# An ifftshift of 8192 x 8192 floats by DMA alone: part of the copies moved to the other queue and cut into 8 KB packets

## The chip, the cores and the metric

The kernel runs on one core of a Trainium2 chip. Its time is the device time in microseconds (us) of one execution, given as the median of several runs. The core has compute engines (none of which this kernel uses for the result), and sixteen DMA engines that move data. Two of the core's instruction streams issue the DMAs here: SyncE (SP in the profile) and ScalarE (ACT). A DMA is split over the sixteen DMA engines; each moves its share in packets, one packet for one contiguous run of bytes. The profile calls the sync engine's queue q1 and the scalar engine's queue q10.

## The reference

```python
def setup_inputs():
    return {"x": np.random.randn(8192, 8192).astype(np.float32)}

def reference(x):
    return np.fft.ifftshift(x)
```

For even sizes this swaps the quadrants: output row r, column c is input row (r + 4096) mod 8192, column (c + 4096) mod 8192. No arithmetic is done. The matrix has 268.44 MB, so the kernel reads and writes 268.44 MB each. A row is 32 KB, half a row 16 KB, and every half row of the output is a contiguous half row of the input.

## The kernel before, in words

The kernel copies from HBM to HBM with DMAs only; `copy` (line 26) works out the source of an output region and issues one DMA for it (line 29) on the queue that it is given. `hr` and `hc` are half the rows and half the columns, `ENGINES` is 16 and `per` is 16, so a block is `rows` = 256 rows and the output has 32 blocks. Of each block the left half (columns 0 to 4095) and the right half are two copies of 4 MB each.

The pattern `back` (line 45) describes a half block as 16 x 16 half rows of 16 KB. Its outer dimension, one step of one row, is what is split over the sixteen DMA engines; its inner dimension goes backward by 16 rows. So engine e copies row e of every group of sixteen rows: at any time the sixteen engines work on about sixteen neighbouring rows, from the block's last group to its first.

The loops (lines 47 to 54) go through the blocks from the last to the first in groups of four. The left halves all go to the sync queue in falling order (line 49). The right halves all go to the scalar queue, with the order in each group of four turned by two (line 50). So each queue carries half of the bytes, in 16 KB packets.

One group of sixteen rows of one right half (`start`, line 36) is copied ahead of the loop, in column strips of 4 KB (lines 38 to 42). The strips are cut at 14, 9 and 4 rows into two DMAs each, so that the sixteen engines get different numbers of 4 KB packets, from one to seven. The scalar queue has seven such small DMAs ahead of its 32 large ones, of which one is a group shorter (`rest`, lines 46 and 52).

The order in which the DMAs are recorded is not yet the order in which they depend on each other. The framework (the tile context) puts the DMAs of both queues into one order of its own, hands eight completion semaphores out in turn along it, and lets each DMA wait, on the engine that issues it, until the DMA eight places earlier in that order has landed. Each engine issues its own DMAs strictly in that order. In the kernel before, the order is the first strip, the first sync DMA, the six other strips, and from there one scalar and one sync DMA in turn, so that after the start each queue has four DMAs outstanding and waits only for its own.

Of the kernel before, what the change touches and what calls it, by code (L numbers as in the profile page):

```python
# [1 line left out]

# [4 lines left out]


ENGINES = 16


@with_exitstack
def kernel(
    ctx: ExitStack,
    tc: tile.TileContext,
    x: bass.AP,
    out: bass.AP,
):
    nc = tc.nc
    R, C = x.shape  # L20
    hr = R // 2
    hc = C // 2
    per = 16
    rows = ENGINES * per

    def copy(queue, row, col, dims):

        src = (row + hr) % R * C + (col + hc) % C
        queue.dma_start(
            out=bass.AP(out.tensor, out.offset + row * C + col, dims),  # L30
            in_=bass.AP(x.tensor, x.offset + src, dims),
        )

    start = R - 3 * rows
    strip = hc // 4
    for n, k in enumerate((14, 9, 4)):
        col = hc + n * strip
        copy(nc.scalar, start + rows - ENGINES, col, [[C, k], [1, strip]])  # L40
        copy(nc.scalar, start + rows - ENGINES + k, col, [[C, ENGINES - k], [1, strip]])
    copy(nc.scalar, start + rows - ENGINES, hc + 3 * strip, [[C, ENGINES], [1, strip]])


    back = [[C, ENGINES], [-ENGINES * C, per], [1, hc]]
    rest = [[C, ENGINES], [-ENGINES * C, per - 1], [1, hc]]
    for first in range(R - 4 * rows, -1, -4 * rows):
        for n in (3, 2, 1, 0):
            copy(nc.sync, first + n * rows + rows - ENGINES, 0, back)
            right = first + (n + 2) % 4 * rows  # L50
            if right == start:
                copy(nc.scalar, right + rows - 2 * ENGINES, hc, rest)
            else:
                copy(nc.scalar, right + rows - ENGINES, hc, back)


# [1 line left out]
_INS = ['x']  # L58
_OUTS = [((8192, 8192), 'float32')]


# [23 lines left out]
```

## Time and profile before

| what | value |
|---|---|
| timed runs | 821.81, 822.63, 822.93 us; median 822.63 |
| the profiled execution: span from the first to the last instruction | 810.9 us |
| what lies around the span, by the median | 11.7 us |
| busy time of compute engines | POOL 0.2 us, four constants that the framework sets |
| DMA issues | sync 32 of 4,096 KB; scalar 31 of 4,096 KB, one of 3,840 KB and seven strips |
| first issue, on both queues | 0.73 us from the span's start |
| one issue instruction | median 571 ns on SP, 578 ns on ACT |
| from issue to landing on the sync queue | median 100.9 us |

The profile is that of one execution; of it the span is known, and the 11.7 us are the difference to the median of the timed runs. The page gives, for forty slices of the span, the mean busy share of the DMA engines (9 is 90% or more) and the GB/s that they copied, and for each queue its packets, its MB and the time of its packets as a share of sixteen engines' span. The view of stretches gives for any window of time its length, the busy time of POOL, the TensorE clock, the DMA share and, in the last column, the GB/s; it counts a packet in the window in which it starts, so that the share can stand a little over 1 in a short window. The records of single packets give the queue, start, duration and size of each, without the engine's number.

### The profile page before, as it was taken

What the parts mean: (1) busy time and instruction counts of PE and PEld (TensorE: products, weight loads), DVE (VectorE), ACT (ScalarE), POOL (GpSimd) and SP (SyncE); (2) the same over time, 40 slices, a digit from 0 to 9 for tenths busy, and PEclk for the clock granted to TensorE, in tenths of its full rate; (3) what the DMA queues carried; (4) which work ended last, traced back from release to release, by engine and by line L of the source; (5) the groups of instructions that cost most, each with busy time, mean ns of one, the idle gap of its engine ahead of it and who ended that gap; (6) DMA issues with size and microseconds to landing.
All of it is one profiled execution on the core that took longest, in us unless ns stands there. A gap on an engine that the chain in (4) does not pass through costs nothing. (4 is left out here: it accounts for less than half of the span.)

```text
span 810.9 us, 116 instructions
## 1 busy us (share of the span) xinstructions
POOL 0.2 (0%) x4
## 2 busy tenths in 40 slices
POOL 0000000000000000000000000000000000000000
DMA  9999999999999999999999999999999999999998
GB/s 302 328 335 329 334 333 331 331 335 330 326 331 329 331 335 330 332 332 337 335 336 333 333 337 330 334 335 331 336 331 333 335 334 335 333 330 336 333 338 296
DMA packets 17520, 268.44 MB, mean 331 GB/s; under 512 B 1088, under 2 KB 1088, under 8 KB 1152
## 3 DMA queue, kind: packets, MB, share of 16 engines
q1 hardware_dynamic: 8704, 134.22, 49.7%
q10 hardware_dynamic: 8816, 134.22, 49.6%
HBM read 268.44 MB, written 268.44 MB: 662 GB/s over the span
## 5 line engine op out<-in xcount | busy, mean ns | idle before, releaser
L69 POOL MEMSET const-bfloat16-1.0<- 128x1 bf16 x1 | 0.1, 102 | 0.0
L69 POOL MEMSET const-uint8-127<- 128x1 uint8 x1 | 0.1, 102 | 0.0
L69 POOL MEMSET const-float32-0.0<- 128x1 f32 x1 | 0.1, 99 | 0.2 <-issue 0.2
L69 POOL MEMSET const-float32-1.0<- 128x1 f32 x1 | 0.1, 99 | 0.0
## 6 DMA issues: line engine op xcount, KB each, us to landing
out_dram<-in_x_dram SPq DMA_DIRECT2D x32, 4096.0 KB, 100.9
out_dram<-in_x_dram ACTq DMA_DIRECT2D x31, 4096.0 KB
out_dram<-in_x_dram ACTq DMA_DIRECT2D x1, 3840.0 KB
out_dram<-in_x_dram ACTq DMA_DIRECT2D x1, 64.0 KB, 10.8
out_dram<-in_x_dram ACTq DMA_DIRECT2D x1, 56.0 KB
out_dram<-in_x_dram ACTq DMA_DIRECT2D x1, 48.0 KB
out_dram<-in_x_dram ACTq DMA_DIRECT2D x1, 36.0 KB
out_dram<-in_x_dram ACTq DMA_DIRECT2D x1, 28.0 KB
```

Source lines behind the costliest of these rows:

```text
L69: nc = _bacc.Bacc("TRN2", target_bir_lowering=False, num_devices=1)
```

## The change

The strips, the groups of four and the pattern `rest` go. The loop now runs over all 32 blocks from the last to the first. The left half of block n is copied as before, by `whole`, on the sync queue. The right half that goes with it is that of the block sixteen further on. When n leaves a remainder of 1 by 3 (11 of the 32 blocks) it is copied by `whole` as well, also on the sync queue. Otherwise (21 blocks) it is copied by `pieces` on the scalar queue: 256 rows in rising order, with the bytes of one packet limited to `piece * 4` = 8 KB, so that each half row is two packets. In the built program such a DMA has the dimensions 256 x 2 x 2048, in which the outermost is split over the engines: engine e gets sixteen rows in a row, e * 16 and on.

```diff
     per = 16
     rows = ENGINES * per
+    blocks = R // rows
+    piece = hc // 2
 
-    def copy(queue, row, col, dims):
-
+    def copy(queue, row, col, dims, **how):
         src = (row + hr) % R * C + (col + hc) % C
         queue.dma_start(
             out=bass.AP(out.tensor, out.offset + row * C + col, dims),
             in_=bass.AP(x.tensor, x.offset + src, dims),
+            **how,
         )
 
+    def whole(block, col):
+        dims = [[C, ENGINES], [-ENGINES * C, per], [1, hc]]
+        copy(nc.sync, block * rows + rows - ENGINES, col, dims)
 
+    def pieces(block):
+        copy(nc.scalar, block * rows, hc, [[C, rows], [1, hc]], max_dma_last_dim=piece * 4)
 
-    start = R - 3 * rows
-    strip = hc // 4
-    for n, k in enumerate((14, 9, 4)):
-        col = hc + n * strip
-        copy(nc.scalar, start + rows - ENGINES, col, [[C, k], [1, strip]])
-        copy(nc.scalar, start + rows - ENGINES + k, col, [[C, ENGINES - k], [1, strip]])
-    copy(nc.scalar, start + rows - ENGINES, hc + 3 * strip, [[C, ENGINES], [1, strip]])
-
-
-    back = [[C, ENGINES], [-ENGINES * C, per], [1, hc]]
-    rest = [[C, ENGINES], [-ENGINES * C, per - 1], [1, hc]]
-    for first in range(R - 4 * rows, -1, -4 * rows):
-        for n in (3, 2, 1, 0):
-            copy(nc.sync, first + n * rows + rows - ENGINES, 0, back)
-            right = first + (n + 2) % 4 * rows
-            if right == start:
-                copy(nc.scalar, right + rows - 2 * ENGINES, hc, rest)
-            else:
-                copy(nc.scalar, right + rows - ENGINES, hc, back)
+    for n in reversed(range(blocks)):
+        right = (n + blocks // 2) % blocks
+        whole(n, 0)
+        if n % 3 == 1:
+            whole(right, hc)
+        else:
+            pieces(right)
```

## The prediction

> **What bounds the kernel now.** I read three views, the page first. Its slices show the sixteen DMA engines busy from end to end and the bytes moving at an almost constant pace:
>
> ```profile
> DMA  9999999999999999999999999999999999999998
> DMA packets 17520, 268.44 MB, mean 331 GB/s; under 512 B 1088, under 2 KB 1088, under 8 KB 1152
> q1 hardware_dynamic: 8704, 134.22, 49.7%
> q10 hardware_dynamic: 8816, 134.22, 49.6%
> HBM read 268.44 MB, written 268.44 MB: 662 GB/s over the span
> ```
>
> No compute engine does anything. The two queues' shares add to 99.3% of sixteen engines, so an engine always has a packet in hand, and one at a time. The second view is the waits of the issuing engine:
>
> ```profile
> SPq L29 <- DMA out_dram<-in_x_dram: 686.8, 28, 28.4
> ```
>
> SP spends the span waiting for its own earlier DMAs. That is back-pressure, not starvation: four 4 MB DMAs per queue are outstanding, and an issue lands a median 100.9 us later while the queue finishes one about every 25 us. So an issue comes some 75 us before its bytes can move, and neither issue time nor the wait is on the path. The third view is the stretches of time:
>
> ```profile
> 3.00:5.00 2.00, 0.00 (x0) 1.00 0.96 393
> 5.00:14.00 9.00, 0.00 (x0) 1.00 1.03 338
> 14.00:23.00 9.00, 0.00 (x0) 1.00 1.02 327
> 30.00:780.00 750.00, 0.00 (x0) 1.00 1.00 333
> 805.50:808.50 3.00, 0.00 (x0) 1.00 0.94 311
> ```
>
> The last column is GB/s copied. In the trace's packet records a 16 KB packet takes 608 to 2346 ns, mean 786; a third of them take the smallest usual time, 611 ns, which on sixteen engines would be 429 GB/s. The steady 333 is therefore set by what the packets meet in memory, not by the engines. What they meet depends on which rows are in hand together: I spread each packet's bytes evenly over its duration and averaged the rate over all 25 us cycles between two completions on the sync queue. It runs from 304 to 362 GB/s with the place in the cycle, with a standard error of about 5 at each place. These two ends are my bounds for any arrangement that this trace does not show.
>
> **What the change really does: the order.** I followed the built order of the changed program, because eight completion semaphores are handed out in that order, and each DMA waits for the one eight places before it. Write A0 to A20 for the scalar DMAs and S0 to S42 for the sync DMAs. The order is A0, S0, A1 to A15, S1, A16 to A20, S2, S3, and so on to S42. So S1 waits for A8, S2 for A14, S3 for A15, S5 to S9 for A16 to A20, and SP issues strictly in order. The two queues are **not** interleaved 2:1 all through. The scalar queue runs first, almost by itself, and then the sync queue runs by itself.
>
> How many bytes move in which company follows from one 16 KB packet going beside one 8 KB packet (the records of before show the queues taking turns packet by packet, with chains of start and end on one engine). A sync DMA is then covered by half a scalar one. S0 and S1 each take half of an A; S2 takes half of A15; S3 and S4 fill A16; S5 to S8 each take half of one of A17 to A20. That makes 9 S and 4.5 A mixed (56.6 MB), 16.5 A alone (69.2 MB), and 34 S alone (142.6 MB). 79% of the bytes move with one queue alone, a state that before is in only at its two ends.
>
> **The terms**, against the profiled span of 810.9 us; the median of the timed runs, 822.63, lies 11.7 us above it, and I add the same 11.7 at the end.
>
> 1. Sync alone, 142.6 MB. The nearest row is 5 to 14 us, where the sync queue moves 16 KB packets beside a few 4 KB ones: 338 by the row, 332 when packets are cut at the window's edges. Bounds 304 and 362, that is +41 and -34 us against 428.2 us at 333. I take 332: **+1.3 us**.
>
> 2. Scalar alone, 69.2 MB. The nearest rows are 14 to 23 us, where the first sync DMA has ended and the second has no packet out yet (327; 322 cut at the edges from 16.5 to 22.3), and the last microseconds, scalar alone (311; 325 cut at the edges). I take 323: 214.2 instead of 207.8 us, **+6.4 us**. At 304 it is +20, at 362 it is -17. The engines' shares of a DMA also lie differently: before, sixteen engines work on sixteen neighbouring rows, 32 KB apart; now each has a block of sixteen rows, so neighbours are 512 KB apart. No row shows that spacing, so it gets the same two ends.
>
> The Trainium skill ("DMA: Bandwidth & Descriptors", section "Latency and other measured facts") states that copies within HBM lose rate with a row pitch at a large power of two: 207 instead of 214 GB/s per direction at 512 KiB, and far more from 2 MiB. Taken over to the spacing of the engines it would be an estimate of 3.4% on the scalar queue's 88.1 MB, +8.9 us in the place of +6.4, and 837 us in all. This trace has no such stretch.
>
> 3. 5,376 half rows become two packets each. From the records, 4 KB takes 159 ns uncontended and 16 KB 611, so a packet has (4 x 159 - 611) / 3 = 8.3 ns that does not grow with its bytes. 5,376 x 8.3 / 16 engines = 2.8 us if all of it shows, nothing if the memory hides it as it hides most of the difference between 611 and 786. I take the middle, **+1.4 us**.
>
> 4. The handover. S8 needs only half of A20's length, so when A20 ends the sync queue is empty, and S9 waits for A20. All engines stand still from their own last byte until A20's slowest has landed (a DMA's sixteen landings at the end of before are spread over 1.5 us, so about 0.8 in the mean), and then for the time from an issue to the first packet (issue at 0.73, first packet at 2.18 us: 1.45), and about 0.1 for the semaphore: **+2.4 us**. Bounds 0, if the packets' turns leave some of S8 over, and 4.
>
> 5. Nothing, with its cover: the seven strips go (0.6 to 1.4 us of issue each on ACT, while the sync queue was feeding all engines). The first packet still comes from an issue at the start. The instructions that issue (0.57 us each, 64 instead of 71) lie beside 12 us and more of data each; without that cover 64 of them on two queues would be under 25 us. The uneven strips gave engines 1 to 7 extra packets of 4 KB; the last landings were spread over 1.5 us, so at most that much comes back at the end, and I count none. ACT now issues eight DMAs ahead instead of four; if its ring cannot take them, only ACT's own issues are delayed, 50 us before they are needed. Each end of a DMA costs the queue one turn, which the other queue fills today; alone, the queue's own next packet should follow its 9 ns semaphore write.
>
> Sum: 810.9 + 1.3 + 6.4 + 1.4 + 2.4 = 822.4, and with 11.7 around it **834 us**, 1.4% slower than before.
>
> **Rivals.**
>
> *The rows collide* (chance 0.24). The 512 KB spacing, or one stream reading one half of each row and writing the other, meets memory as in the bad part of the cycle. For: around the end of a sync DMA the engines hold about thirteen scalar packets to three, and the rate falls to 304 to 318. Against: the 327 of 14 to 23 us. Scalar alone at 304 gives 834 + 13 = 847; both alone at 304 give 834 + 13 + 40 = 887.
>
> *One stream is better than two* (0.25; this one is faster than before). If packets of two unrelated row groups hinder one another, the lone sync queue runs freer: after the handover all engines restart together on sixteen neighbouring rows, as at launch. For: 393 from 3 to 5 us, and about 365 around the end of a scalar DMA, where thirteen packets of sixteen are the sync queue's. Against: the rate falls to 338 and below as soon as the launch is over, with the sync queue still nearly alone. At 362 the 142.6 MB take 394 instead of 429.5 us: 798 us; with the scalar part at 362 too, 775. It wins as soon as the lone sync queue holds more than 341 GB/s, which repays the 10.2 us of the other terms.
>
> *Company does not matter* (0.09). All bytes go at 333 in whatever queue, and only terms 3 and 4 are left: 826; if these too are hidden, 823, no change. The flat slices speak for it, the 304 to 362 within a cycle against it. The Trainium skill (same page, section "Issuing engines are not separate DMA queues") says the same as a rule: DMAs from different engines end on the same sixteen DMA engines and interleave, and a second issuing engine saves only issue time. The launch row of 338 agrees with it, the cycle does not.
>
> That the diff fails to bring the interleaving it describes is no rival here but part of the forecast. Were the queues after all to run 2:1, it would be term 3 alone, about 824.
>
> **How the numbers follow.** Forecast 0.42 (826 to 845), collision 0.24, one stream 0.25, no matter 0.09. A measurement of this kernel can tell about 0.2% from no change, 1.6 us. Faster: 0.25. Same: 0.06, the hidden part of the last rival. Slower: 0.42 + 0.24 + 0.03 = 0.69. The range of 792 to 874 leaves out the better half of the one-stream case below its 798, and the collision of both queues toward 887; the forecast's own range is 826 to 845.
>
> **What would show it.** Right order: q1 holds about 180 MB and q10 88 MB, with 10,752 packets of 8 KB on q10; ACT's issues all come in the first half, and SP's second one only after some 100 us; SP waits for DMAs for most of the first half. Handover: one dent in the DMA slices near the middle. Terms 1 and 2: GB/s of the slices at about 332 in the second half and 323 in the first. The forecast is wrong if the lone sync half stands above 341 or below 320, or if the queues share the whole span.

## The result and the profile after

The changed kernel takes 832.81 us (median of 4 runs, 828.19 to 834.8), the kernel before 822.78 beside it. The ratio is 1.0117, 95% interval 1.008 to 1.0153: slower by about 10 us. In a later set (experiment e7 below) it was 829.67 beside 821.42, ratio 1.0101 (1.0071 to 1.0131).

The page of the profile after, span 829.4 us:

```profile
DMA  8999999999999999998999999999999999999998
GB/s 297 320 328 325 332 325 327 330 317 333 330 328 331 327 323 331 324 326 290 318 320 314 329 319 330 322 327 331 329 325 327 326 327 327 323 332 329 327 328 292
DMA packets 22784, 268.44 MB, mean 324 GB/s; under 512 B 1024, under 2 KB 1024, under 8 KB 1024
...
q1 hardware_dynamic: 11696, 180.36, 65.7%
q10 hardware_dynamic: 11088, 88.08, 33.0%
HBM read 268.44 MB, written 268.44 MB: 647 GB/s over the span
```

The engines still have a packet in hand nearly all the time, so the loss is one of pace and of one hole. Of the bytes, two thirds are on q1 and one third on q10, as the diff says. The nineteenth slice (373 to 394 us) has the hole: 8 instead of 9, and 290 GB/s; the slices behind it stay at 314 to 330 for a while. The waits of the sync engine show the order (us in total, times, longest):

```profile
SPq L33 <- DMA out_dram<-in_x_dram: 382.1, 8, 131.1
```

and so do the issues in the view of line 33 (shortest, median and longest issue in ns, first and last start in us):

```profile
L33 SPq DMA_DIRECT2D out_dram<-in_x_dram x43: 571/11591/29097, 0.7 to 750.6; - x43
L33 ACTq DMA_DIRECT2D out_dram<-in_x_dram x21: 662/12602/37307, 0.7 to 269.4; - x21
```

SP waits in eight places only, once for 131 us: it holds one DMA and then stands until the scalar queue's A8 has landed. All scalar issues start in the first 270 us. In the packet records the scalar queue is alone for about 211 us and moves 68.6 MB in that time, both move for about 172, and the sync queue is alone from 389 us to the end.

One number of the prediction's base has to be read anew. Every timed run of the changed kernel stands 1.8 us above its own span, and so does the kernel before when it is profiled again (e0: 824.29 beside 822.5). With the same 1.8 us, the 810.9 us of the profile before belong to an execution of about 812.7 us (worked out, not measured), faster than any of its timed runs; not 11.7 us but 1.8 lie around a span. The sum was made of differences and then set upon the median, so it is not shifted by this. But 333 GB/s is the pace of that one execution; e0 has 327 to 329.

### The profile page after: what moved, and what is told of

It reads as the page before. It is cut to its first block, busy times and chain, and to the rows that moved or that the text cites. A ratio compares the mean times of both kernels' runs of the same rounds, so it can differ in the third digit from the quotient of the medians.

```text
span 829.4 us, 109 instructions
## 1 busy us (share of the span) xinstructions
POOL 0.2 (0%) x4
## 3 DMA queue, kind: packets, MB, share of 16 engines
q1 hardware_dynamic: 11696, 180.36, 65.7%
q10 hardware_dynamic: 11088, 88.08, 33.0%
```

## The experiments

All ratios are to the kernel before, run on the same chip in the same set, with their 95% interval. There are three sets, each on a chip of its own: e0 to e3, e4 to e7, e8 to e11. Each stretch that is shown is from one profiled execution of its version. The experiments that keep or change the order do it with edges between the DMAs that order them in the program and add no wait:

```diff
+        if issued:
+            tc.add_manual_dep(
+                dma.ins, issued[-1].name,
+                mybir.DependencyInfo(mybir.DependencyClass.NoSync, mybir.DependencyReason.DATA),
+                reason="order",
+            )
+        issued.append(dma.ins)
```

### e0: the kernel before against itself

No edit.

> The kernel before, unchanged, against itself. The profile that the prediction worked from had a span of 810.9 us, while the timed runs of the changed kernel stand only 1.8 us above their spans, so the 810.9 belongs to an execution of about 812.7 us, some 10 us under the median of 822.8. Theory: executions of this kernel scatter by about 1%, and a new profile will show a span of 815 to 825 us and a steady rate of 327 to 331 GB/s. Rival: 11.7 us do lie around the span of this kernel, and the new span is 811 again. Ratio to before: 1.000 within 0.003.

Measured: 822.56 us, ratio 1.0006 (0.9991 to 1.0021), span 822.5 of an execution of 824.29 us. The theory holds: executions of one kernel scatter by a few us, and the first profile lies outside them on the fast side. No run shows why.

### e1: the changed kernel in its written order

The edges above, and nothing else; the built order is then S0, S1, S2, A0, S3, A1 and so on.

> The changed kernel, its DMAs kept in the order in which they are written, by ordering edges that add no wait: the sync and the scalar queue then run beside each other 2:1 from start to end. Theory of the prediction (what costs is that one queue runs alone for four fifths of the bytes, and the gap at the handover): time falls from 832.8 by about 3.2 us of gap and by 5 to 8 us of pace, to 820 to 825 us, ratio to before 0.997 to 1.003; no dent in the slices. Rival (the 8 KB packets or the 512 KB spacing of the engines cost it, in whatever order): 829 to 834 us, ratio 1.008 or more. Rival (mixed sizes keep the engines out of step and help): under 815.

Measured: 822.5 us, ratio 1.0009 (0.9998 to 1.002). The theory of the prediction holds as far as the order goes, and both rivals fall: with the same packets, the same spacing and the same bytes on each queue, the order alone gives the whole loss back. Its slices have no hole:

```profile
DMA  8999999999999999999999999999999999999998
GB/s 305 326 330 326 325 331 328 329 336 324 333 330 334 325 331 335 324 328 327 332 328 329 329 327 330 332 327 328 334 326 331 329 330 333 329 327 331 330 326 299
```

### e2: the sync queue alone

```diff
-        if n % 3 == 1:
-            whole(right, hc)
-        else:
-            pieces(right)
+        whole(right, hc)
```

> All 64 half blocks in 16 KB packets on the sync queue alone; nothing on the scalar queue, no strips, no 8 KB packets, no handover. Theory (a lone queue has the pace of the second half of the changed kernel, 325.7 GB/s): 824 us of moving, span 829, time 830, ratio about 1.010. Rival (the loss of the changed kernel comes from the scalar queue's part, and a lone queue of whole half rows is as fast as two): 820 to 824, ratio 1.000. Rival (one stream is better than two): below 815.

Measured: 824.3 us, ratio 1.0035 (1.002 to 1.0051). Between the theory (1.010) and the first rival (1.000): a lone queue costs about 2.5 us over the whole matrix, a third of what the pace of the changed kernel's second half would make it. The 325.7 GB/s of the changed kernel's second half were not the pace of a lone queue.

### e3: 16 KB packets in the changed kernel

```diff
-        copy(nc.scalar, block * rows, hc, [[C, rows], [1, hc]], max_dma_last_dim=piece * 4)
+        copy(nc.scalar, block * rows, hc, [[C, rows], [1, hc]])
```

> The changed kernel without the limit of 8 KB: the scalar queue moves the same rows in the same engine blocks, in 16 KB packets, in the same built order. Sync DMAs issued beside A15 to A20 are then covered one to one, so that the sync queue still has one left when A20 ends and the gap at the handover should close. Theory: minus 1.4 us (0 to 2.8) for the packets and minus 3 for the gap, 828 to 829 us, ratio 1.005 to 1.008, no dent near the middle. Rival (8 KB packets are most of the loss): 823 or less. Rival (8 KB packets help by keeping engines out of step): 834 or more.

Measured: 823.57 us, ratio 1.0028 (1.0012 to 1.0044), no hole. Lower than the theory expected, near the first rival. But the edit does two things, since one sync packet now takes as long as one scalar packet and the gap closes. The next set takes them apart.

### e4: the gap alone

The changed kernel's built order, written out as a string and kept by the edges, with S2 ahead of A20 (a is a scalar, s a sync DMA). Without the exchange the string would end in `"aaaaa" + "s" * 41`:

```diff
...
+    order = "as" + "a" * 15 + "s" + "aaaa" + "sa" + "s" * 40
```

> The changed kernel in its own built order, with one exchange: S2 stands ahead of A20, so that S9 no longer waits for A20 and the sync queue still has a DMA when the scalar queue ends. All else stays: 8 KB packets, the scalar queue mostly alone and then the sync queue alone. Theory (the gap of about 3 us is one term among others, the rest is the 8 KB packets with no 16 KB packets beside them): time falls by 3 us from that of the changed kernel on the same chip, ratio to before 1.007 to 1.009. Rival (the gap and what hangs on it, such as engines that drift apart before it, is all that separates the changed kernel from the version with 16 KB packets): ratio 1.003. Rival (the gap's end in step pays itself back): ratio unchanged at 1.012.

Measured: 824.34 us, ratio 1.0043 (1.0027 to 1.0059); the changed kernel beside it (e7) 829.67. The exchange also lets S2 start 12 us earlier, at 209.7 us. It is worth 5.3 us by the medians and 4.8 by the two ratios, whose intervals leave about 2 to 7.6. The theory, 1.007 to 1.009, misses; the first rival holds: the gap and what hangs on it is nearly all that parts the changed kernel from its 16 KB version. The stretches of the changed kernel show what hangs on it (start:end in us, length, POOL, clock, DMA share, GB/s):

```profile
384.00:386.00 2.00, 0.00 (x0) 1.00 1.05 319
386.00:388.00 2.00, 0.00 (x0) 1.00 0.36 131
388.00:390.00 2.00, 0.00 (x0) 1.00 0.47 115
390.00:392.00 2.00, 0.00 (x0) 1.00 0.70 279
392.00:395.00 3.00, 0.00 (x0) 1.00 1.11 399
...
395.00:445.00 50.00, 0.00 (x0) 1.00 1.00 317
445.00:600.00 155.00, 0.00 (x0) 1.00 1.00 325
600.00:800.00 200.00, 0.00 (x0) 1.00 1.00 327
```

and the same stretches of e4, which moves nearly the same blocks at these times, without the gap:

```profile
380.00:395.00 15.00, 0.00 (x0) 1.00 1.00 327
395.00:445.00 50.00, 0.00 (x0) 1.00 0.99 328
445.00:600.00 155.00, 0.00 (x0) 1.00 1.00 329
600.00:800.00 200.00, 0.00 (x0) 1.00 1.00 328
```

The hole itself is 2.7 us of all engines (their idle time between 382 and 398 us in the packet records; 2.7 in e7's profile too). The restart runs at 399 GB/s for 3 us by the row, 366 when packets are cut at the edges, and then falls to 305, or 312. From 395 to 445 us the changed kernel has 317 (319 in e7) where e4 has 328, and to 600 us 325 (323) where e4 has 329. With the packets cut at the edges, 395 to 600 us is 323.4 and 322.0 beside 328.5: 205 us x (328.5 - 322.7) / 328.5 = 3.6 us. Hole and slow stretch make 6.3 us by these profiles, against the 5.3 and 4.8 of the times; e7's profile is that of its slowest run.

### e5 and e6: the scalar queue alone, 8 KB and 16 KB

```diff
-        whole(n, 0)
...
+        pieces(n, 0)
+        pieces(right, hc)
```

with the column as a second argument of `pieces`; e6 also leaves out the limit of 8 KB.

> All 64 half blocks on the scalar queue alone, in 8 KB packets and in the engine blocks of sixteen rows; no sync queue, no handover. Theory (8 KB packets cost something only when no 16 KB packet goes beside them): the changed kernel's loss that is neither gap (3) nor lone pace (2) is about 5 us on 69 MB, so 20 us on 268 MB beyond a lone queue of 16 KB packets: 840 to 847 us, ratio 1.02 to 1.03. Rival (a packet costs its fixed 8.3 ns and no more): 824.3 + 5.6 = 830, ratio 1.010. Rival (nothing, the memory hides it): 824, ratio 1.003.

> The same with 16 KB packets: one queue, engines 512 KB apart. Beside the version on the sync queue alone (engines 32 KB apart, ratio 1.0035) it gives the price of the spacing. Theory by the 322.8 GB/s of the lone scalar stretch of the 16 KB version: 268.4 / 322.8 gives 832 us of moving and 838 us, ratio 1.019. Rival (spacing does not matter here, the stretch was only its rows): 824, ratio 1.003.

Measured: e5 824.66 us, ratio 1.0038 (1.002 to 1.0057); e6 824.81 us, ratio 1.0041 (1.0021 to 1.006). In both the rival that expected no difference is right. (The other rival of e5 has its sum too low: 16,384 half rows x 8.3 ns / 16 engines are 8.5 us, not 5.6; e5's interval leaves out either.) 8 KB against 16 KB packets: nothing that these intervals can tell. Engines 512 KB apart (e6) against 32 KB apart (e2): nothing either, though e2 also uses the other queue and was run in another set. The lone queues cost 2.5 to 3.4 us, alike within the intervals. Where, the stretches of the kernel before profiled again (first), of e2 (second) and of e5 (third) show:

```profile
10.00:60.00 50.00, 0.00 (x0) 1.00 1.00 327
60.00:200.00 140.00, 0.00 (x0) 1.00 1.00 329
...
600.00:800.00 200.00, 0.00 (x0) 1.00 1.00 327
```

```profile
10.00:60.00 50.00, 0.00 (x0) 1.00 1.00 320
60.00:200.00 140.00, 0.00 (x0) 1.00 1.00 328
...
600.00:800.00 200.00, 0.00 (x0) 1.00 1.00 330
```

```profile
10.00:60.00 50.00, 0.00 (x0) 1.00 0.99 320
60.00:200.00 140.00, 0.00 (x0) 1.00 1.00 323
...
600.00:800.00 200.00, 0.00 (x0) 1.00 1.00 330
```

Late in the span the lone queues are as fast as two. They lose in their first 60 to 200 us, after the start from standstill, with figures like those of the changed kernel behind its gap (e6 has 313 and 323 in the first two stretches). By these rows the two stretches cost e2 an estimated 1.5 us and e5 3.6. So a lone queue is not slower as such; a lone queue that has just started is. The profiles of e5 and e6 are of runs 2 to 3 us above their medians; that of e2 is at its median.

### e7: the changed kernel again

No edit.

> The changed kernel itself, on the same chip as the three others, so that differences of a few us can be told. Ratio to before 1.0117 within 0.003, and a gap of about 3 us where the scalar queue ends.

Measured: 829.67 us, ratio 1.0101 (1.0071 to 1.0131), gap 2.7 us.

### e8 to e11: are the engines in step?

A new theory: sixteen engines that start together on equal packets move in step and hinder one another, until they have drifted apart. The kernel before cuts seven strips at its launch that give its engines unequal work. In e8, with the built order written out as in e4 but without the exchange, one group of rows of S10 is cut like that behind the gap (S starts the block, + is a strip, r the rest of the block), in e11 one of A0 at the launch too:

```diff
...
+    order = "as" + "a" * 15 + "s" + "aaaaa" + "s" * 8 + "S++s++s+++r" + "s" * 30
```

e9 puts the strips between the first DMAs of e2 in the same way, and e10 takes them out of the kernel before:

```diff
-    for n, k in enumerate((14, 9, 4)):
...
-            if right == start:
-                copy(nc.scalar, right + rows - 2 * ENGINES, hc, rest)
-            else:
-                copy(nc.scalar, right + rows - ENGINES, hc, back)
+            copy(nc.scalar, right + rows - ENGINES, hc, back)
```

> The changed kernel with its gap, but one group of rows of S10 is cut into the seven uneven 4 KB strips of the kernel before, spread between S9, the two next sync DMAs and the rest of S10. New theory: sixteen engines that start together on equal packets are in step and move some 2% less until they have drifted apart (318 and 317 GB/s in the 50 us after the gap in the two profiles of the changed kernel, 322 to 323 over the 205 us from 395 us, beside 328.5 without the gap); the strips put them out of step within some 35 us. So the 2.8 us of the gap stay, most of the 3.6 us behind it go: ratio 1.007 to 1.0085, and 327 or more GB/s from 445 us on. Rival (the slow stretch belongs to the rows or to the restart itself, not to the step): ratio 1.010 to 1.012 and 320 to 325 until 600.

> The sync queue alone, 16 KB packets, with the same seven strips between its first DMAs. Theory (in step at the launch: 321 GB/s in the first 50 us, 326 in the next, 328 to 330 later): without strips 1.0035, with them 1.001 to 1.002, and at least 328 GB/s from 60 us on. Rival (a lone queue is slower as such): 1.0035 as without them.

> The kernel before without its strips: two queues, one to one, all packets 16 KB, all engines in step at the launch. Theory: the launch in step costs two equal queues as it costs one, ratio 1.002 to 1.004, and 320 to 325 GB/s in the first 50 us. Rival (two queues keep the engines out of step by themselves): ratio 1.000 within 0.0015.

> The changed kernel with its gap and strips in both places, at the launch (on the scalar queue, as before) and behind the gap. Theory: what is left beside the kernel before is the idle gap of 2.8 us and a rest of at most 1 to 2 us, ratio 1.0035 to 1.006. Rival (8 KB packets, spacing or the lone queues do cost something of their own): 1.008 or more.

Measured: e8 828.53 us, ratio 1.0072 (1.005 to 1.0094); e9 823.06, 1.0027 (1.0007 to 1.0047); e10 822.41, 1.0006 (0.9989 to 1.0024); e11 827.76, 1.0064 (1.0045 to 1.0082). The stretches behind the gap, e8 first and e11 second:

```profile
395.00:445.00 50.00, 0.00 (x0) 1.00 1.00 325
445.00:600.00 155.00, 0.00 (x0) 1.00 1.00 330
600.00:800.00 200.00, 0.00 (x0) 1.00 1.00 329
```

```profile
395.00:445.00 50.00, 0.00 (x0) 1.00 0.99 319
445.00:600.00 155.00, 0.00 (x0) 1.00 1.00 325
600.00:800.00 200.00, 0.00 (x0) 1.00 1.00 327
```

e8's ratio is where the theory put it, e11's a little above (its interval takes in the theory and, just, the rival's 1.008). By its stretches e8 looks as the theory wants it, and e11 with the same strips in the same place looks like the changed kernel. e9's interval takes in both its theory and its rival. e10's ratio is where its rival put it, that two equal queues need no strips; but its interval just reaches the theory's 1.002, and its 325 GB/s from 10 to 60 us is the upper end of what the theory gave. The spread of the sixteen engines' landings of one DMA (their standard deviation) doesn't help the theory either: from 395 to 445 us its mean is 0.39 us in the changed kernel and 0.44 in e4, for 318 and 329 GB/s. So it stays open why a queue that restarts alone is slow for 150 to 200 us. What the pair e4 and e7 shows is that it is, and that the gap brings it about. Whether the strips save any of the slow stretch is not settled: the intervals of e8 and e11 overlap that of e7 (1.0071 to 1.0131, another set), and of the two profiles, which disagree, e8's is of a run near its fastest (826.46 us) and e11's of its slowest (829.0). None of the versions is faster than the kernel before beyond its interval.

## Why the prediction was right, point by point

834 us were forecast, 832.81 and in the second set a ratio that makes 831 were measured. The order, the handover and the state of the queues were right. Of the four terms, 2 and 3 were too high and 4 too low. That these errors largely cancelled is luck: the total was met more closely than its parts.

- **The order** (right). S1 is issued at 132.6 us, S2 at 222.0, S9 at 388.3; q1 has 180.36 MB, q10 88.08 and 10,752 packets of 8 KB. The scalar queue moves 68.6 MB alone, where 69.2 were worked out. e1 shows that the order is the cause: without it the ratio is 1.0009.
- **Terms 1 and 2, the lone queues, +7.7 us together** (mechanism half right, size too high). e2 to e6 give 1.8 to 3.4 us, the three lone queues 2.5 to 3.4. The sign named for the two terms, about 332 GB/s in the second half and 323 in the first, did not come. The stretches of the changed kernel are level:

```profile
30.00:340.00 310.00, 0.00 (x0) 1.00 0.99 328
400.00:810.00 410.00, 0.00 (x0) 1.00 1.00 326
```

e7 has 325 and 324 there, e0 329 and 328. So the lone scalar queue was not the slow part, and term 2, with 6.4 us the largest, had the wrong size. From 22 to 136 us, where that queue is alone, the changed kernel has 326, e7 322 and e0 329; an estimate from these for 69.2 MB is 2 to 4.6 us. The rows that priced the two terms, 5 to 14 us, 14 to 23 us and the last microseconds, were short and beside the launch or the end (the last packets of the first sync DMA reach to 18.7 us, into the second of them); what they showed was the slow start, not a lasting pace. The 512 KB spacing, which had the bounds -17 and +20, costs nothing that shows here. With it falls, for this pattern, the estimate that was drawn from the Trainium skill ("DMA: Bandwidth & Descriptors", section "Latency and other measured facts"): on all bytes, as in e6, it would be 3.4% more than in e2, but e6 is at 1.0041 and e2 at 1.0035.
- **Term 3, 8 KB packets, +1.4 us** (too high). Its lower bound, nothing, is what e5 against e6 and e1 against the kernel before give, within their intervals. That the fixed 8.3 ns of a packet are hidden by its wait in memory is argued, not shown; the records leave room for it: 8 KB packets take 407 ns in the mean, where the smallest usual time is 309.
- **Term 4, the handover, +2.4 us, bounds 0 and 4** (mechanism right, size too low). The standstill is 2.7 us, close to what was worked out. With what hangs on it the term is 5.3 us by the medians, since the lone queue that restarts is slow for some 200 us. That is over its upper bound, though the intervals (about 2 to 7.6 us) do not rule out less. That a standstill has an after-effect was not thought of; the launch showed it (393 GB/s from 3 to 5 us in the row, 296 from 8 to 10 us in the packet records) and was read as a lone stream's pace.
- **Term 5** (right in its sum). e10 without the strips is at 1.0006, so no loss from them shows beside two queues. ACT's issues did become long, with a median of 12.6 us, but so did SP's with 11.6, which was not thought of. Neither shows as idle time of the DMA engines outside the hole.
- **The rivals.** "The rows collide" found no support: over 50 us and more the lone queues run at 313 to 333 GB/s, not at 304. "One stream is better than two" falls by e2 (1.0035). "Company does not matter" is nearer to the truth than its chance of 0.09: once under way, one queue and two move 325 to 330 GB/s alike; but it missed the slow start. The Trainium skill (same page, section "Issuing engines are not separate DMA queues") has it as a rule that a second issuing engine saves only issue time, and these rates agree with it.

The sum as the runs give it: about 3 us for lone queues with the gap closed (e4), 2.7 us for the hole and 2.6 us behind it, 8.3 us in the second set; the first set has 10.0 with an interval of 6.6 to 12.6.

## What to carry to other kernels

Follow the built order of the instructions and the semaphores that tie them before you believe what a loop says about which transfers run beside each other: here an interleaving that stands in the source was not in the program, and edges that keep the written order gave the 1% back. Where a queue hands over to another, see that the second has a transfer outstanding before the first ends; the hole cost about twice its own length by the medians, 5.3 us for 2.7. And price a state from rows that lie in that state for long: ten microseconds beside a launch told the sign here, but not the size.

## What the runs showed of the hardware that was not expected

- After a standstill of all sixteen engines, a lone queue moves 399 GB/s for 3 us (366 with the packets cut at the edges, 370 in e7), 305 for the next 5, and 317 to 325 for the 200 us that follow, where without the standstill it moves 328. Why is open.
- Issue instructions are not always short. In the kernel before their median is 0.57 us. In the changed kernel ACT's, with 8 KB packets, took a median of 12.6 us and up to 37.3, and SP's, with 16 KB packets, 11.6 and up to 29.1. A lone queue had fewer than the eight DMAs under way that the semaphores would allow: from issue to landing one of 16 KB packets has a median of 81.1 us in e2 and in e6, and one of 8 KB packets 56.6 us in e5, at one 4 MB DMA every 13 us. Late in the span these queues still moved 330 GB/s.
- Executions of one kernel on one chip scatter by several us (the kernel before: 819.26 to 824.75 in 35 runs), and one profile, of a run of about 812.7 us by its span, lies outside. Differences under 1% need many runs, and the pace of a single profile is no norm.
